# Layer 0's even pairs form and split the token difference themselves; pair 2 multiplies gate and up in turns

## The chip, the core and the metric

The kernel runs on one core of one Trainium2 chip. The metric is the device time of one execution in microseconds (us); smaller is better. The engines of the core work side by side and wait for each other by semaphores: TensorE (PE, matrix products, with its weight loads as PEld), VectorE (DVE), ScalarE (ACT), GpSimd (POOL), and SyncE (SP), which here only issues DMA transfers.

## The reference, cut to what matters

A two-layer decoder trunk on x of 512 tokens by 1024 features, all float32: a Mamba-2 mixer, a ConvFFN, shared keys and values, differential attention, a second ConvFFN. The change lies in the ConvFFN of both layers, and in one preparation for the keys that runs beside layer 0's.

```python
def causal_dwconv(u, w, b):            # width 3 over tokens
    ...
def conv_ffn(x, ln_g, up_w, conv_w, conv_b, down_w):
    u = causal_dwconv(rms_norm(x, ln_g) @ up_w, conv_w, conv_b)
    gate, up = u[..., :FFN_DIM], u[..., FFN_DIM:]
    return (jax.nn.silu(gate) * up) @ down_w      # FFN_DIM = 2816
def shared_kv(x, kv_ln_g, kv_w, k_norm_g):
    kv = rms_norm(x, kv_ln_g) @ kv_w
    ...
```

## The kernel before, in words

**Precision.** Every float32 operand is split into a high part (ACT copies it to the rounded matmul type) and a low part (DVE subtracts the high part from the value). A product is three matmuls: high by high, high by low, low by high (lines 246 to 248 for the plain products, 1437, 1439 and 1434 for layer 0's down products). The helper `pieces` (ACT at line 1083, DVE at 1084) splits a stream operand. A weight chunk is loaded to a raw buffer by SP (lines 175 and 177), its high part cast by ACT (line 185, or 1276 for down weights), its low part formed by DVE (196 or 1277). High and low weights have three buffers each. A chunk is prepared two uses ahead.

**The FFN.** The 2816 hidden columns are 22 blocks of 128, which the code calls pairs, because each has a gate block and an up block; two pairs, an even and an odd one, make a double. `PARTS_D` divides the 22 into parts of 6, 8 and 8. A part's pairs are multiplied first, and its part of the down product follows while the next part's first pairs are under way; the last part's down product ends the layer's FFN. `KINDS` says which doubles are plain (P) and which use a scheme of seven products for the up projection (S); `STEPS` is the order of the work in a part (D is the down product of the part before). In layer 0's last part the two pairs 20 and 21 come last, and the down product behind them.

**The head of an FFN.** Pairs 0 and 1 multiply the stream before it is normalised, since the norm isn't ready yet, and what comes out is scaled afterwards (`evac`, line 1468). Their weights come in two chunks, one with rows 0 to 3 of the gate and the up block, one with rows 4 to 7 of both, so that gate and up are multiplied in turns, row by row (`p < WHOLE` in `whole` and `ffn_plan`); a chunk is then loaded by two DMAs of 256 KB. From pair 2 on a chunk is a whole gate block or a whole up block, by one DMA of 512 KB: 8 rows of the gate first, then 8 rows of the up block. A row's product is the three matmuls above; its stream operands are `xgh` and `xgl`. Pair 2 is the first that needs the normalised stream, which is formed (line 1092) and split (1083, 1084) in four quarters: rows 0 and 2, 1 and 3, 4 and 6, 5 and 7. The splits write over the stream that pair 1 reads, so the quarters with rows 4 to 7 can only be split when pair 1 has used those rows.

**Behind a pair.** `tapped` forms the width-3 convolution of gate and up (ACT 1066, DVE 1068) and SiLU (ACT 1473), `gated` multiplies them (DVE 1160), and `operands` makes of a double's two results, each cut into token halves, the seven stream operands of the down product: e0 and e1 are the even pair's halves, o0 and o1 the odd pair's. Operand 0 is e0, operands 1 and 2 are o0 and o1, operand 3 is e0 - e1, operand 4 is o1 - e1, and 5 and 6 are two further sums. The even pair splits operand 0; all others are formed (lines 1314 to 1317) and split with the odd pair. For the last double of an 8-pair part they stand in the tiles sEh and sEl.

**The down product of layer 0** (`down_features`) runs the seven products in the order 5, 1, 2, 6, 7, 4, 3 (`SEVEN[0]`), which use operands 3, 0, 1, 6, 4, 5 and 2. Each has two weight chunks, and each chunk uses all doubles of the part, the last double last in each half.

**Key staging** (`stage`, called after the steps of pairs 3, 4 and 5 and after each step of the later parts but D): eight times a block of the key weights is loaded by SP to the one buffer `stage` (line 1005), scaled by ACT in two halves (1011), and stored by ACT's queue to a scratch tensor (1012). A load is asked for at one call, scaling and store two calls later, the next load two calls after that.

**Order.** PE's instructions run as they are written. The order on ACT, DVE and SP is set when the program is built, by a planner that works from estimates of its own and puts an instruction ahead of its place in the code where an engine would be free; at run time each engine and each queue works strictly in that order.

Of the kernel before, what the change touches and what calls it, by code (L numbers as in the profile page):

```python
# [31 lines left out]
PARTS_D = (0, 6), (6, 14), (14, 22)  # L32
KINDS = "PPP", "PSPP", "PPPP"
STEPS = "PPPPPPPPPPPP", "PPDPPP51P26P734PPPPP", "PPDPPPPPPPPPPPPPP"
WHOLE = 2
SEVEN = "5126743", "1257634"
AH = 8
EPS = 1e-6
# [7 lines left out]
def trunk_kernel(ctx: ExitStack, tc, x, ssm_ln_g, ssm_in_w, ssm_conv_w, ssm_conv_b, ssm_dt_bias,  # L46
# [4 lines left out]
    act, dve, pool, pe, sync = nc.scalar, nc.vector, nc.gpsimd, nc.tensor, nc.sync  # L51
# [18 lines left out]
    def w_cols(w, k0, nk, c0, ncol):  # L70
        return w[k0 * P:(k0 + nk) * P, c0:c0 + ncol].rearrange("(k p) c -> p k c", p=P), nk, ncol
# [40 lines left out]
    def down_plan(l, i):  # L112
        p0, p1 = PARTS_D[i]
        nq = (p1 - p0) // 2
        for m in SEVEN[l]:
            for c in range(0, nq, 2) if l else range(2):
                plan.append(("s%d%s_%d_%d" % (l, m, p0, c), (l, m, p0, c, min(2, nq - c) if l else nq)))

    def ffn_plan(l):
        w = ffn_up_w[l].rearrange("(k p) (j c) -> p k j c", p=P, j=2)  # L120
        for i in range(len(PARTS_D)):
            for kind, p, n in up_order(i):
                if kind == "D":
                    down_plan(l, i - 1)
                elif kind == "P" and p >= WHOLE:
                    plan.append(("h%d_%d_%d" % (l, p, n), *w_cols(ffn_up_w[l], 0, KB, n * FFN + p * P, P)))
# [110 lines left out]
    def chunk(key):  # L237
        while state["next"] <= state["use"] + AHEAD and state["next"] < len(plan):
            emit_chunk()
        state["use"] += 1  # L240
        k, h, l = ready.pop(0)
        assert k == key, (k, key)
        return h, l
# [396 lines left out]
    with tc.tile_pool(name="ssm_y", bufs=1) as yp, tc.tile_pool(name="ssm", bufs=1) as sp:  # L640
# [29 lines left out]
        with tc.issue_after(b1_end.ins):  # L670
            for c in range(NT):
# [11 lines left out]
                          in1=dtb.unsqueeze(1).to_broadcast([P, NT, NH]), op=ALU.add)  # L683
# [7 lines left out]
        for n in (13, 11, 9, 7, 5, 3):  # L691
# [6 lines left out]
                                 in1=alog.unsqueeze(1).to_broadcast([P, NT, NH]),  # L698
# [151 lines left out]
        def out_proj(g, yh, yl, norm):  # L850
            for c in range(4):
                wh, wl = chunk("out%d_%d" % (g, c))
                for i in range(2):
                    m = 2 * c + i
                    ps = mm_bank("ps_o%d_%d" % (g, m))
                    for k in range(4):
                        state["last"] = mm3(ps, wh[:, k, i * P:(i + 1) * P], wl[:, k, i * P:(i + 1) * P],
                                            yh[k], yl[k], k == 0, k == 3)
                    add_to_stream(m, ps, 16, norm)
                    yield  # L860
# [83 lines left out]
        for g in range(NG):  # L944
# [40 lines left out]
            else:  # L985
                op = out_proj(g - 1, *prev, None)
# [27 lines left out]
    def bias_ranges(pl, behind):  # L1014
        pl = pl.rearrange("p a t -> p (a t)")
        rb = pl[:AH, :32]
        pool.tensor_copy(rb[:, 0:1], behind[:AH, 0:1])
        pool.dma_start(rb, rel_bias.rearrange("b h -> h b"))
        pool.tensor_scalar(out=rb, in0=rb, scalar1=-1.0, scalar2=None, op0=ALU.mult)
        hb = NBIAS // 2  # L1020
        for i in range(2):
            bv = pl[:AH, 32 + i * hb:32 + (i + 1) * hb]
            if i:
                pool.memset(bv[:, hb - (P - 1):], FAR)
            for b, a, e in _ranges():
                a, e = max(NBIAS - e - i * hb, 0), min(NBIAS - a - i * hb, hb)
                if a < e:
                    src = rb[:, 0:e - a][:, ::-1] if b == 0 else rb[:, b:b + 1].to_broadcast([AH, e - a])
                    pool.tensor_copy(bv[:, a:e], src)
            pool.dma_start(bd[:, i * hb:(i + 1) * hb], bv)  # L1030

    def ffn(l, norm, bp, gnext, nnext):
        with (tc.tile_pool(name="ffn_h%d" % l, bufs=1) as hp, tc.tile_pool(name="ffn%d" % l, bufs=1) as fp,
# [3 lines left out]
            def whole(p, pss):  # L1037

                pss += [(aux_bank if j else mm_bank)("ps_%s%d_%d" % ("gu"[j], l, p)) for j in range(2)]
                for c in range(2):  # L1040
                    wh, wl = chunk("h%d_%d_%d" % (l, p, c))
                    if p >= WHOLE:
                        for k in range(KB):
# [30 lines left out]
            def u_tile(name):  # L1074
                return fp.tile([P, 2, T], F32, tag="u", name=name, bufs=2)
# [4 lines left out]
            sub = ALU.subtract  # L1080

            def pieces(hi, lo, v):
                act.activation(hi, v, AF.Copy)  # L1083
                dve.tensor_tensor(out=lo, in0=v, in1=hi.bitcast(F32), op=sub)  # L1084
# [74 lines left out]
            def gated(p, ga, up, sides):  # L1159
                dve.tensor_tensor(out=ga, in0=ga, in1=up, op=ALU.mult)  # L1160
                operands(p, ga, sides)
# [87 lines left out]
            def down_ahead(p0, n, ks, eng=sync):  # L1249
                for k in ks:  # L1250
                    for c in range((n // 2 + 1) // 2 if l else 2):
                        down_load(p0, n, k, c, eng)
# [40 lines left out]
            def operands(p, ga, sides):  # L1293

                h = ga.rearrange("p (i t) -> p i t", i=2)
                if p % 2 == 0:
                    if any(p == p1 - 2 and p1 - p0 == 8 for p0, p1 in PARTS_D):
                        sh, sl = (flat(t)[:, :7 * 256].rearrange("p (s t) -> p s t", s=7) for t in sE)
                    else:
                        sh = hp.tile([P, 7, 256], F32R, tag="sh", name="sh%d" % p, bufs=3)  # L1300
                        sl = hp.tile([P, 7, 256], F32R, tag="sl", name="sl%d" % p, bufs=3)
                    sides[p] = (sh, sl, h)
                    pieces(sh[:, 0], sl[:, 0], h[:, 0])
                    return
                sh, sl, e = sides[p - 1]
                pieces(sh[:, 1:3], sl[:, 1:3], h)
                e0, e1, o0, o1 = e[:, 0], e[:, 1], h[:, 0], h[:, 1]
                if l:
                    dve.tensor_tensor(out=o1, in0=e1, in1=o1, op=sub)
                    dve.tensor_tensor(out=e1, in0=e0, in1=e1, op=sub)  # L1310
                    dve.tensor_tensor(out=e0, in0=o1, in1=e0, op=sub)
                    dve.tensor_tensor(out=o0, in0=o0, in1=e0, op=ALU.add)
                else:
                    dve.tensor_tensor(out=e0, in0=e0, in1=e1, op=sub)
                    dve.tensor_tensor(out=e1, in0=o1, in1=e1, op=sub)
                    dve.scalar_tensor_tensor(out=o1, in0=o1, scalar=-1.0, in1=e0, op0=ALU.mult, op1=sub)
                    dve.scalar_tensor_tensor(out=o0, in0=o1, scalar=-1.0, in1=o0, op0=ALU.mult, op1=sub)
                pieces(sh[:, 3:5], sl[:, 3:5], e)
                pieces(sh[:, 5:7], sl[:, 5:7], h)

            def down_tokens(p0, n, sides, last):
# [149 lines left out]
            def tapped(p, us):  # L1471
                ga = taps(0, p, us[0])
                act.activation(ga, ga, AF.Silu)
                return ga, taps(1, p, us[1])
# [3 lines left out]
            def stage():  # L1478

                staged["at"] += 1  # L1480
                if staged["v"] and staged["at"] > 1:
                    key_weights_out(*staged["v"])
                    staged.update(v=None, at=0)
                elif not staged["v"] and staged["n"] < KB and staged["at"] > 1:
                    staged.update(v=key_weights_in(fp, staged["n"]), n=staged["n"] + 1, at=0)

            def plain(p, sides):

                pss = []
                for _ in whole(p, pss):  # L1490
                    yield
                sides["open"] = p, tapped(p, pss)

            def gate(sides):
                p, (ga, up) = sides.pop("open")
                gated(p, ga, up, sides)
                return ga
# [27 lines left out]
            for p in range(2, 6):  # L1525
                for _ in plain(p, sides):
                    if p > 2:
                        next(sums, None)
                        if not l:
                            stage()  # L1530
                if p == 2:
                    gated(1, *tapped(1, (u1[:, 0], u1[:, 1])), sides)
                ga = gate(sides)
                next(sums, None)
                if p == 3:
                    down_ahead(*parts[0], "z")
                if not l and p == 3:
                    bias_ranges(u_tile("ranges"), ga)
# [59 lines left out]

    norm_kv = Norm(bp, "kv")
    ffn(0, norm, bp, None, norm_kv)  # L1600


    norm1 = Norm(bp, "f1")
    with tc.tile_pool(name="att", bufs=1) as ap, ExitStack() as later:
# [353 lines left out]
        with tc.manual_schedule(engines={mybir.EngineType.PE}):  # L1958
# [49 lines left out]
            last_out(norm1)  # L2008

    ffn(1, norm1, bp, None, None)  # L2010


# [34 lines left out]
```

## Time and profile before

| | us |
|---|---|
| median of 3 runs | 1326.8 (1326.25 to 1327.58) |
| profiled execution, its own time | 1327.54 |
| its span, first to last instruction | 1325.8 |
| mean granted PE clock | 0.996 |
| busy: PE, DVE, ACT, POOL | 1310.4, 1062.4, 735.7, 173.5 |

The page gives the span, each engine's busy time, and groups of instructions by line. Waits are listed as "who waited <- for whom: us in total, times, longest". In a timeline the columns are start (us from the span's start), duration, engine, line, operation, output <- inputs, shapes, count, and in brackets the idle time before it with what ended it. Matmuls overlap in their pipeline: the work of one is the distance of two starts, not its duration. In a row of the view by stretches the columns are the stretch, its length, then busy time (and count) of PE, PEld, DVE, ACT and POOL, the granted PE clock, the DMA share and GB/s.

### The profile page before, as it was taken

How to read it: one execution, taken by the hardware profiler on the slowest of the kernel's cores; microseconds unless marked ns; L12 is line 12 of the kernel's file. 1: busy time of each engine (PE TensorE's matmuls, PEld its weight loads, DVE VectorE, ACT ScalarE, POOL GpSimd, SP SyncE). 2: the span in 40 equal slices, each digit the busy share in tenths (PEclk: the TensorE clock that was granted, in tenths of full speed). 3: DMA queues.
4: the chain of work that ended last, by engine and by line, in shares of the span. 5: the costliest groups of instructions: out<-in, count | busy, mean ns of one | idle time of the engine just before them, and what ended most of it. 6: DMA issues, size and time to landing. Idle time of an engine off the chain costs nothing.

```text
span 1325.8 us, 18563 instructions
## 1 busy us (share of the span) xinstructions
PE 1310.4 (99%) x6915; PEld 1104.2 (83%) x6915; DVE 1062.4 (80%) x1769; ACT 735.7 (55%) x1203; POOL 173.5 (13%) x204
## 2 busy tenths in 40 slices
PE   9999999999999999999999999999999999999998
PEld 8878888888887898899879888777887889888887
DVE  7889888789879976975766968677779977977776
ACT  6696554742466644643444667777556535643442
POOL 5330300200120420020011310000020020020001
PEclk9999999999999999999998999999999999999999
DMA  7553433532365796377345573221133494466335
GB/s 208 161 153 96 142 105 108 139 95 72 110 193 178 175 239 138 116 135 195 96 95 113 170 163 111 75 69 65 51 117 103 107 235 112 128 112 190 95 64 127
DMA packets 200218, 171.01 MB, mean 129 GB/s; under 512 B 7804, under 2 KB 174080, under 8 KB 200128
## 3 DMA queue, kind: packets, MB, share of 16 engines
q1 hardware_dynamic: 169424, 120.73, 30.6%
q0 software_dynamic: 27248, 43.80, 17.2%
q10 hardware_dynamic: 3456, 5.30, 1.1%
q8 instruction: 54, 0.88, 0.3%
q14 instruction: 36, 0.29, 0.1%
HBM read 163.36 MB, written 6.44 MB: 128 GB/s over the span
## 4 chain that ended last, share of the span: by engine, by line
PE 94%; DVE 2%; issue 1%; ACT 1%; DMA 0%; POOL 0%; SPq 0%; DVEq 0%; POOLq 0%; ACTq 0%
PE ps_u L246 5%; PE ps_u L247 5%; PE ps_u L248 5%; PE ps_g L247 5%; PE ps_g L248 5%; PE ps_g L246 5%; PE ps_in L246 5%; PE ps_in L248 5%; PE ps_in L247 5%; PE ps_s L1434 3%; PE ps_s L1439 3%; PE ps_s L1437 3%; PE ps_s L1333 3%; PE ps_s L1338 3%; PE ps_s L1336 3%; PE ps_o L247 2%
## 5 line engine op out<-in xcount | busy, mean ns | idle before, releaser
L196 DVE TENSOR_TENSOR wl_h<-wr_h,wh_h 128x1024 fp32r<-128x1024 f32 x80 | 98.3, 1229 | 45.2 <-ACT wh_h L185 42.5
L247 PE MATMUL ps_g<-xgl,wh_h 128*128 128x512 f32 x320 | 125.7, 393 | 3.6 <-DVE xgl L1084 3.6
L185 ACT ACTIVATE wh_h<-wr_h 128x1024 fp32r<-128x1024 f32 x80 | 84.6, 1058 | 78.1 <-PE ps_u L247 28.5
L246 PE MATMUL ps_g<-xgh,wh_h 128*128 128x512 f32 x320 | 125.6, 393 | 0.8 <-ACT xgh L1083 0.8
L248 PE MATMUL ps_g<-xgh,wl_h 128*128 128x512 f32 x320 | 125.2, 391 | 0.0
L246 PE MATMUL ps_u<-xgh,wh_h 128*128 128x512 f32 x320 | 124.6, 389 | 0.0
L247 PE MATMUL ps_u<-xgl,wh_h 128*128 128x512 f32 x320 | 124.5, 389 | 0.0
L248 PE MATMUL ps_u<-xgh,wl_h 128*128 128x512 f32 x320 | 124.5, 389 | 0.0
L246 PE MATMUL ps_in<-xgh,wh_in 128*128 128x512 f32 x304 | 122.9, 404 | 0.0
L248 PE MATMUL ps_in<-xgh,wl_in 128*128 128x512 f32 x304 | 119.7, 394 | 0.0
L247 PE MATMUL ps_in<-xgl,wh_in 128*128 128x512 f32 x304 | 119.1, 392 | 0.0
L1238 POOL DMA_DIRECT2D wz<-in_ffn_down_w_dram x36 | 44.0, 1237 | 497.9 <-DVE wl_s L1277 415.8
L247 PEld LDWEIGHTS ps_g<-xgl,wh_h 128*128 128x128 f32 x320 | 60.4, 189 | 17.1 <-DVE xgl L1084 4.9
L1276 ACT ACTIVATE wh_s<-wz 128x1024 fp32r<-128x1024 f32 (+2 forms) x42 | 41.5, 989 | 57.0 <-PE ps_s L1338 19.2
L246 PEld LDWEIGHTS ps_g<-xgh,wh_h 128*128 128x128 f32 x320 | 60.4, 189 | 13.8 <-ACT xgh L1083 1.6
L1083 ACT ACTIVATE sh<-vg 128x512 fp32r<-128x512 f32 (+1 forms) x72 | 40.3, 572 | 55.8 <-DVE vg L1160 38.3
L248 PEld LDWEIGHTS ps_g<-xgh,wl_h 128*128 128x128 f32 x320 | 60.5, 189 | 12.5
L247 PEld LDWEIGHTS ps_u<-xgl,wh_h 128*128 128x128 f32 x320 | 60.1, 188 | 12.5
L246 PEld LDWEIGHTS ps_u<-xgh,wh_h 128*128 128x128 f32 x320 | 60.2, 188 | 12.4
L248 PEld LDWEIGHTS ps_u<-xgh,wl_h 128*128 128x128 f32 x320 | 60.1, 188 | 12.4
L248 PEld LDWEIGHTS ps_in<-xgh,wl_in 128*128 128x128 f32 x304 | 57.1, 188 | 12.2 <-issue 0.4
L246 PEld LDWEIGHTS ps_in<-xgh,wh_in 128*128 128x128 f32 x304 | 57.2, 188 | 11.7 <-issue 1.3
(508 smaller groups left out, 3607.7 us busy)
## 6 DMA issues: line engine op xcount, KB each, us to landing
wr_h<-in_ffn_up_w_dram SPq DMA_DIRECT2D x72, 512.0 KB, 3.9
wr_in<-in_ssm_in_w_dram SPq DMA_DIRECT2D x40, 512.0 KB, 3.9
wz<-in_ffn_down_w_dram POOLq DMA_DIRECT2D x29, 512.0 KB, 5.9
m<-cumd POOLq DMA_DIRECT2D x16, 512.0 KB, 4.3
wr_out<-in_ssm_out_w_dram SPq DMA_DIRECT2D x16, 512.0 KB, 3.5
wr_s<-in_ffn_down_w_dram SPq DMA_DIRECT2D x13, 512.0 KB, 3.9
wr_h<-in_ffn_up_w_dram SPq DMA_DIRECT2D x16, 256.0 KB, 3.5
stage<-in_kv_w_dram SPq DMA_DIRECT2D x8, 512.0 KB, 3.9
```

Of the source, the lines that this page charges most:

```text
L185: return act.activation(self.wh[:, :self.n], self.raw[:, :self.n], AF.Copy)
L196: return eng.tensor_tensor(out=self.wl[:, :self.n], in0=self.raw[:, :self.n], in1=self.wh[:, :self.n].bitcast(F32), op=ALU.subtract)
L246: pe.matmul(ps, wh, xh, start=start, stop=False)
L247: pe.matmul(ps, wh, xl, start=False, stop=False)
L248: return pe.matmul(ps, wl, xh, start=False, stop=stop).ins
L1083: act.activation(hi, v, AF.Copy)
L1238: state["plus"] = pool.dma_start(view(t, nq), source(p0, c, nq, j, i), accum_op=ALU.add).ins
L1276: act.activation(wh[:, :n], t[:, :n], AF.Copy)
L1333: pe.matmul(pss[b], h, ws[q][1][:, cols], start=False, stop=end and q == qs[-1], skip_group_check=more)
L1336: pe.matmul(pss[b], h, ws[q][0][:, cols], start=first and q == qs[0], stop=False, skip_group_check=more)
L1338: pe.matmul(pss[b], w, ws[q][0][:, cols], start=False, stop=False, skip_group_check=more)
L1434: pe.matmul(v[:, b], wl[:, q, cols], h, start=False, stop=q == nq - 1, skip_group_check=not opens or b > 0)
```

## The change

`WHOLE` goes from 2 to 3: pair 2 of both layers takes its weights in the form of pairs 0 and 1, rows 0 to 3 of gate and up, then rows 4 to 7, multiplied in turns. In layer 0 an even pair forms e0 - e1 in place, once operand 0 is split, and splits it as operand 3; the odd pair no longer forms it and splits operand 4 alone. Layer 1's operands stay. The calls of `stage` behind pair 3's two steps go, so that each staging step comes two calls later in the code.

```diff
-WHOLE = 2
+WHOLE = 3
...
                     sides[p] = (sh, sl, h)
                     pieces(sh[:, 0], sl[:, 0], h[:, 0])
+                    if not l:
+                        dve.tensor_tensor(out=h[:, 0], in0=h[:, 0], in1=h[:, 1], op=sub)
+                        pieces(sh[:, 3], sl[:, 3], h[:, 0])
                     return
...
                 else:
-                    dve.tensor_tensor(out=e0, in0=e0, in1=e1, op=sub)
                     dve.tensor_tensor(out=e1, in0=o1, in1=e1, op=sub)
...
-                pieces(sh[:, 3:5], sl[:, 3:5], e)
+                if l:
+                    pieces(sh[:, 3:5], sl[:, 3:5], e)
+                else:
+                    pieces(sh[:, 4], sl[:, 4], e1)
                 pieces(sh[:, 5:7], sl[:, 5:7], h)
...
                     if p > 2:
                         next(sums, None)
-                        if not l:
+                        if not l and p > 3:
                             stage()
```

## The prediction, made before the changed kernel was run

> **What bounds the kernel now.** The page comes first: TensorE (PE) is busy in all but 15.4 us of the span, so only PE's gaps and the matmuls that run slowly beside them can be won.
>
> ```profile
> span 1325.8 us, 18563 instructions
> PE 1310.4 (99%) x6915; PEld 1104.2 (83%) x6915; DVE 1062.4 (80%) x1769; ACT 735.7 (55%) x1203; POOL 173.5 (13%) x204
> ```
>
> Then PE's waits (engine, line, releaser: total, times, longest):
>
> ```profile
> PE ps_s L1437 <- ACT sEh L1083: 4.8, 1, 4.8
> PE ps_g L247 <- DVE xgl L1084: 3.6, 3, 1.9
> PE ps_g L246 <- ACT xgh L1083: 0.8, 2, 0.5
> PE ps_s L1439 <- DVE sEl L1084: 0.2, 1, 0.2
> ```
>
> These are 9.4 us in two kinds of place: the last down product of layer 0, and the third pair (pair 2) of each layer. The timeline of PE shows that they cost more than their length. First the down product:
>
> ```profile
> 691.89 0.28 PE L1437 MATMUL ps_s<-sh,wh_s 128*128 128x256 f32 x1
> ...
> 697.58 0.58 PE L1437 MATMUL ps_s<-sEh,wh_s 128*128 128x256 f32 x1 [4.82 <-ACT sEh L1083]
> ...
> 699.63 0.41 PE L1437 MATMUL ps_s<-sh,wh_s 128*128 128x256 f32 x1
> 699.84 0.41 PE L1439 MATMUL ps_s<-sl,wh_s 128*128 128x256 f32 x1
> ...
> 704.51 0.29 PE L1437 MATMUL ps_s<-sh,wh_s 128*128 128x256 f32 x1
> ...
> 707.39 0.28 PE L1437 MATMUL ps_s<-sh,wh_s 128*128 128x256 f32 x1
> ...
> 710.27 0.28 PE L1437 MATMUL ps_s<-sh,wh_s 128*128 128x256 f32 x1
> ```
>
> A weight chunk is 24 matmuls here. Undisturbed it takes 710.27 - 707.39 = 2.88 us, 0.12 each. The row at 704.51 opens the second half of the second chunk, so 36 matmuls lie before it: 4.32 us of work took 12.62. **Lost: 8.30 us**, of which 4.82 and 0.23 are waits; the rest is matmuls at 0.21 instead of 0.12 for some 6 us behind the wait.
>
> Now pair 2, in layer 0 and, last two rows, in layer 1:
>
> ```profile
> 399.56 0.39 PE L246 MATMUL ps_g<-xgh,wh_h 128*128 128x512 f32 x1
> ...
> 402.84 0.50 PE L246 MATMUL ps_g<-xgh,wh_h 128*128 128x512 f32 x1 [0.29 <-ACT xgh L1083]
> 404.24 0.50 PE L247 MATMUL ps_g<-xgl,wh_h 128*128 128x512 f32 x1 [0.89 <-DVE xgl L1084]
> ...
> 407.12 0.74 PE L247 MATMUL ps_g<-xgl,wh_h 128*128 128x512 f32 x1 [1.92 <-DVE xgl L1084]
> ...
> 408.08 0.63 PE L246 MATMUL ps_g<-xgh,wh_h 128*128 128x512 f32 x1
> 408.50 0.63 PE L247 MATMUL ps_g<-xgl,wh_h 128*128 128x512 f32 x1
> ...
> 410.64 0.39 PE L246 MATMUL ps_u<-xgh,wh_h 128*128 128x512 f32 x1
> ...
> 999.10 0.39 PE L246 MATMUL ps_g<-xgh,wh_h 128*128 128x512 f32 x1
> ...
> 1006.34 0.39 PE L246 MATMUL ps_u<-xgh,wh_h 128*128 128x512 f32 x1
> ```
>
> A chunk is 24 matmuls again; what it takes undisturbed is seen in pair 4's up chunk, which isn't alternated, and in pair 1's second chunk, which multiplies gate and up in turns:
>
> ```profile
> 432.43 0.39 PE L246 MATMUL ps_u<-xgh,wh_h 128*128 128x512 f32 x1
> 437.87 0.39 PE L246 MATMUL ps_g<-xgh,wh_h 128*128 128x512 f32 x1
> ...
> 394.12 0.39 PE L246 MATMUL ps_g<-xgh,wh_h 128*128 128x512 f32 x1
> ```
>
> Both last 5.44 us (432.43 to 437.87, 394.12 to 399.56), so taking turns costs PE nothing. Pair 2's gate chunk lasted 11.08 in layer 0 and 7.24 in layer 1. **Lost: 5.64 and 1.80 us.** All that the change can win is 8.30 + 5.64 + 1.80 = 15.74 us.
>
> **The even pair's difference.** The down products of layer 0 go in the order 5, 1, 2, 6, 7, 4, 3. Product 5 takes operand 3, which needs the even pair alone, but before it is split together with operand 4, which needs the odd one. In the rows of DVE and ACT:
>
> ```profile
> 686.49 0.43 DVE L1314 TENSOR_TENSOR vg<-vg 128x256 f32<-128x256 f32 x1
> ...
> 696.38 1.15 ACT L1083 ACTIVATE sEh<-vg 128x512 fp32r<-128x512 f32 x2 [2.80 <-DVE vg L1160]
> ...
> 701.57 1.06 ACT L1276 ACTIVATE wh_s<-wx 128x1024 fp32r<-128x1024 f32 x1 [1.78 <-PE ps_s L1439]
> ```
>
> The difference (L1314) is there at 686.9, the split waits for pair 21's product (L1160) until 696.4. In the new kernel operand 3 can be split right behind L1314, and even behind the weight casts that stand there it is done by about 689, before PE arrives at 691.9. Product 1 (operand 0) is the even pair's too, so the odd pair is first wanted by product 2, after 4 chunks, at 691.9 + 11.5 = 703.4; its splits begin at 696.4 and have 6 us of room. What is late next is the weight cast of the fourth chunk (ACT at 701.57, then its low half on DVE). Before the change it waits for PE to free a buffer, which now happens 7 us earlier (about 694.3); PE wants it at 691.9 + 8.6 = 700.5. If ACT holds it behind the pair's last split, which ends about 699.4, cast and low half end at 701.6 and PE waits 0.1 to 0.5. I take 0.2: **a gain of 8.1**, bounds 7.5 and 8.3.
>
> The price is two splits of 256 columns for one of 512, in 11 double pairs of layer 0:
>
> ```profile
> L1083 ACT ACTIVATE sh<-vg 128x512 fp32r<-128x512 f32 x27 | 16.3, 625 | 21.3 <-DVE vg L1160 11.2 <-DVE vg L1317 7.1 <-DVE vg L1315 3.0
> L1083 ACT ACTIVATE sh<-vg 128x256 fp32r<-128x256 f32 x9 | 3.7, 410 | 7.7 <-DVE vg L1160 7.7
> L1084 DVE TENSOR_TENSOR sl<-vg,sh 128x512 fp32r<-128x512 f32 x27 | 18.1, 687 | 2.1 <-ACT sh L1083 1.9
> L1084 DVE TENSOR_TENSOR sl<-vg,sh 128x256 fp32r<-128x256 f32 x9 | 3.8, 421 | 1.0 <-ACT sh L1083 1.0
> ```
>
> 2 x 410 - 625 = 195 ns on ACT, 2 x 421 - 687 = 155 on DVE: 2.1 and 1.7 us over the layer. Arithmetic is only moved. The cover is the room ahead of PE, here of a weight cast in the steady part:
>
> ```profile
> 653.92 1.05 ACT L185 ACTIVATE wh_h<-wr_h 128x1024 fp32r<-128x1024 f32 x1
> ...
> 664.69 0.39 PE L246 MATMUL ps_u<-xgh,wh_h 128*128 128x512 f32 x1
> ```
>
> A cast begins when a chunk ends (653.8 here) and is for the third chunk after it (two more are ready in their buffers), so it ends 9.7 us before PE takes it. The even pair's new split waits on ACT for L1314, which waits for DVE, and behind it stand such casts; a wait of a microsecond or two there is covered. I cost it at 0; without that cover it would be the 0.4 us of the split and its wait, 11 times.
>
> **Pair 2 in turns.** Pair 2 is the first that multiplies the normalised stream, whose second half is split while the first is in use. Before, rows 4 to 7 are wanted after 12 matmuls (2.7 us), now after 24 (5.44). In layer 0 that is 405.0, and row 5's low part, the second matmul of its group, at 406.6. The DVE rows, and the weight casts that follow:
>
> ```profile
> 405.85 1.22 DVE L1084 TENSOR_TENSOR xgl<-wx,xgh 128x1024 fp32r<-128x1024 f32 x1
> ...
> 411.55 1.22 DVE L196 TENSOR_TENSOR wl_h<-wr_h,wh_h 128x1024 fp32r<-128x1024 f32 x1 [1.48 <-ACT wh_h L185]
> ...
> 435.13 1.22 DVE L196 TENSOR_TENSOR wl_h<-wr_h,wh_h 128x1024 fp32r<-128x1024 f32 x1
> ```
>
> The second xgl ends at 407.07: 0.5 us of the 5.64 stays. In layer 1 nothing stays: the wait that ended at 1004.39 was the last, and there row 5 is wanted at 1005.9. The loads become two of 256 KB for one of 512, pair 2's alone, as pairs 0 and 1 have them.
>
> But PE then runs 5.1 us ahead of a DVE that has no air:
>
> ```profile
> 411.00:436.00 25.00, 25.00 (x112) 20.68 (x111) 23.78 (x36) 18.96 (x28) 1.36 (x1) 1.00 0.61 189
> ```
>
> DVE (fourth figure) is busy 23.8 of 25 us. The cast at 435.13 is pair 5's gate; it ends at 436.35, and PE wants it with the third matmul, 437.87 + 0.45 = 438.3: a room of 1.95 us, the smallest of the stretch. With PE 5.1 ahead 3.2 are missing. DVE gets back the 1.48 it idled before 411.55 (that buffer is freed when pair 2's first chunk ends, at 405 now), and little else: a wait of 1.7 there, with the bounds 0 and 3.2. So **layer 0's head wins 5.64 - 0.5 - 1.7 = 3.4**, bounds 1.9 and 5.6; **layer 1's 1.8**. Were operand 3 still late, the first down product would now wait as the last did; the first part covers it.
>
> **Key staging.** The same 8 loads, 16 scalings and 8 stores come two steps later in the code. They run far ahead of their place (between 356 and 436 us), wherever ACT and SP are free:
>
> ```profile
> 400.50 1.34 ACT L1011 ACTIVATE stage<-stage,c 128x512 f32<-128x512 f32 x2 [3.70 <-DMA stage<-in_kv_w_dram]
> ```
>
> ACT stood 3.70 us before this one for a load, and the second half's splits stood behind it. If the move takes it away, the 0.5 above goes too and DVE gains about 1 us; if it puts such a wait ahead of a cast with less room, up to 2 are lost. Nearest to the row that moves nothing: 0.
>
> **The sum.** 8.1 + 3.4 + 1.8 = 13.3 us, bounds 9 and 15.7. The profiled execution took 1327.54 (span 1325.8 and 1.7 around it), 0.7 above the median of 1326.8; its sum gives 1314.2, and from the median 1313.5, which I take.
>
> [...] After 402.84 three waits of 3.10 us in all, the longest 1.92, left the matmuls at 0.42 instead of 0.227 until 410.64, 1.5 us more. [...]
>
> **Rivals.**
> - DVE takes the head's win back. Pair 5's wait is 3.2, with slow matmuls behind it (1.5): 5.64 - 0.5 - 3.2 - 1.5 = 0.4, total 10.3, 1316.5; with a second such wait 1319. For it speak DVE's 95%, against it the wait's own relief for DVE. Chance 0.19.
> - The wait moves within the last down product: ACT works its queue in order, and the fourth chunk's cast lands behind all splits of pair 21 and DVE's low half behind them; 3 to 4 us of wait and slow matmuls stay, 1318. Against it: ACT is idle for 2.8 us before 696.38. Chance 0.11.
> - Operand 3 is still not ready, because its split is placed with the odd pair's after all: only the heads win, 5.2 us, 1321.6. Against it: L1314 was already placed 9 us ahead. Chance 0.05.
> - Slower: the moved key staging makes ACT stand as at 400.50, 3.70 us for each of its 8 loads, all in the head, where casts have 1.95 us of room and DVE can make up nothing. Each hold is then a PE wait of 1.75 with 1.5 us of slow matmuls behind it: 8 x 3.25 = 26 us against the 13.3 won, 1339.5. It decides from the fifth hold. Against it: the four waits of ACT for these loads were 7.0 us in all, and only one met PE:
>
> ```profile
> ACT stage L1011 <- DMA stage<-in_kv_w_dram: 7.0, 4, 3.7
> ```
>
> Chance 0.06.
>
> **How the numbers follow.** The forecast (11 to 15.7 us won) has 0.59 and lies between 1311 and 1316; the range 1310.5 to 1319.5 takes in the first rival and part of the second. About 0.2% (2.7 us) is what a measurement here can tell from none: faster 0.90, within 0.04, slower 0.06.
>
> **What would show it.** Right: no wait at L1437, the first five chunks of the last down product 2.88 us apart, layer 1's pair 2 in 10.9 us. A wait of PE on wl_h L196 at pair 5 shows the DVE limit; a gate chunk of pair 2 in layer 0 still waiting over 1 us, or a wait of PE on wh_s or wl_s, would make it wrong.

## The result and the profile after

The changed kernel takes 1316.95 us (median of 6 runs, 1314.89 to 1319.12), the kernel before in the same comparison 1327.15 (6 runs, 1326.25 to 1328.08): a ratio of 0.9923 [0.991, 0.9936], 10.2 us won. The forecast was 1313.5, a win of 13.3, so 3.1 us of the win are missing: the time lies inside the range (1310.5 to 1319.5) but just outside the forecast's 1311 to 1316. The profiled execution took 1319.12, the longest of the six.

The page of the changed kernel, then its view of PE's waits:

```profile
span 1317.4 us, 18596 instructions
...
PE 1307.8 (99%) x6915; PEld 1103.0 (84%) x6915; DVE 1061.9 (81%) x1780; ACT 738.8 (56%) x1214; POOL 174.7 (13%) x204
```

```profile
PE ps_g L248 <- DVE wl_h L196: 3.0, 1, 3.0
...
PE ps_s L1341 <- DVE vu L1068: 0.4, 1, 0.4
...
PE ps_g L247 <- DVE xgl L1084: 0.3, 1, 0.3
```

The 4.8 us at the last down product are gone, and of the third pair's 4.4 us (xgl and xgh) 0.3 is left. A wait of 3.0 on the low part of a weight chunk is new, and a small one in layer 1's first down product. (Lines behind 1300 moved by up to five: 1437, 1439 and 1473 of before are 1442, 1444 and 1478 here.)

**The last down product** runs without a gap. The timeline of PE:

```profile
692.84 0.28 PE L1442 MATMUL ps_s<-sh,wh_s 128*128 128x256 f32 x1
...
693.55 0.28 PE L1442 MATMUL ps_s<-sEh,wh_s 128*128 128x256 f32 x1
...
697.15 0.28 PE L1442 MATMUL ps_s<-sh,wh_s 128*128 128x256 f32 x1
...
698.60 0.28 PE L1442 MATMUL ps_s<-sh,wh_s 128*128 128x256 f32 x1
```

From 692.84 to 698.60 lie two chunks: 5.76 us, 2.88 each. Operand 3 (sEh at 693.55) is there in time, and the timelines of ACT and DVE show why: the even pair's difference ends at 687.8, its high part at 688.7, its low part at 690.0. The fourth chunk's cast follows on ACT at 695.43, ahead of the odd pair's splits:

```profile
688.34 0.40 ACT L1083 ACTIVATE sEh<-vg 128x256 fp32r<-128x256 f32 x1
...
695.43 1.06 ACT L1276 ACTIVATE wh_s<-wx 128x1024 fp32r<-128x1024 f32 x1 [0.89 <-PE ps_s L1444]
697.81 0.63 ACT L1083 ACTIVATE sEh<-vg 128x512 fp32r<-128x512 f32 x1 [1.31 <-DVE vg L1160]
```

```profile
687.37 0.42 DVE L1305 TENSOR_TENSOR vg<-vg 128x256 f32<-128x256 f32 x1
688.47 1.23 DVE L1277 TENSOR_TENSOR wl_s<-wz,wh_s 128x1024 fp32r<-128x1024 f32 x1 [0.68 <-ACT wh_s L1276]
689.61 0.42 DVE L1084 TENSOR_TENSOR sEl<-vg,sEh 128x256 fp32r<-128x256 f32 x1
```

**The head of layer 0** wins its time and gives it back. PE at pair 2's leftover wait, and then at pair 5's gate chunk:

```profile
406.94 0.50 PE L247 MATMUL ps_g<-xgl,wh_h 128*128 128x512 f32 x1 [0.32 <-DVE xgl L1084]
...
436.33 0.80 PE L248 MATMUL ps_g<-xgh,wl_h 128*128 128x512 f32 x1 [3.01 <-DVE wl_h L196]
436.93 0.63 PE L246 MATMUL ps_g<-xgh,wh_h 128*128 128x512 f32 x1
...
442.05 0.55 PE L246 MATMUL ps_g<-xgh,wh_h 128*128 128x512 f32 x1
442.43 0.40 PE L247 MATMUL ps_g<-xgl,wh_h 128*128 128x512 f32 x1
```

From 436.33 to 442.43 PE makes 14 matmuls in 6.10 us; undisturbed they take 14 x 0.227 = 3.18. So the place costs 3.01 of wait and 2.92 of slow matmuls, 5.9 us. Matmul by matmul PE stands 5.2 us ahead of the kernel before when pair 2 is over, and 0.9 behind it after this place.

Who was late there? DVE first, then ACT:

```profile
430.35 1.22 DVE L1084 TENSOR_TENSOR sOl<-wz,sOh 128x1024 fp32r<-128x1024 f32 x1
434.45 0.69 DVE L1160 TENSOR_TENSOR vg<-vg,vu 128x512 f32<-128x512 f32 x1 [2.88 <-ACT vg L1478]
435.06 1.22 DVE L196 TENSOR_TENSOR wl_h<-wr_h,wh_h 128x1024 fp32r<-128x1024 f32 x1
```

```profile
427.24 1.06 ACT L185 ACTIVATE wh_h<-wr_h 128x1024 fp32r<-128x1024 f32 x1 [0.61 <-PE ps_g L247]
428.21 0.76 ACT L1066 ACTIVATE vg<-ps_g,cf 128x512 f32<-128x512 f32 x1
432.56 1.34 ACT L1011 ACTIVATE stage<-stage,c 128x512 f32<-128x512 f32 x2 [3.59 <-DMA stage<-in_kv_w_dram]
433.81 0.61 ACT L1478 ACTIVATE vg<-vg 128x512 f32<-128x512 f32 x1
```

Read it backwards. The weight chunk's low part (L196 at 435.06) stands on DVE behind the product of pair 3 (L1160), which waits for pair 3's SiLU (L1478 on ACT). The convolution that it takes is done at 429.8 (DVE), but in ACT's queue the last key scaling stands ahead, and its load isn't there: ACT stands for 3.59 us. There is one buffer `stage`, so a load waits for the store before it; SP could issue this one only at 426.63, and the scaling started 5.9 us later (SPq marks the issue of a transfer):

```profile
426.63 0.37 SPq L1005 DMA_DIRECT2D stage<-in_kv_w_dram  x1
```

In the kernel before, ACT had the last scaling behind the SiLU:

```profile
431.58 0.63 ACT L1473 ACTIVATE vg<-vg 128x512 f32<-128x512 f32 x1 [1.46 <-DVE vg L1068]
...
435.07 1.34 ACT L1011 ACTIVATE stage<-stage,c 128x512 f32<-128x512 f32 x2 [0.42 <-DMA stage<-in_kv_w_dram]
```

So DVE was not short of time here. It idled for 2.88 us:

```profile
411.00:436.00 25.00, 22.32 (x99) 18.16 (x97) 22.11 (x35) 17.47 (x27) 0.50 (x1) 0.99 0.73 214
```

DVE (fourth figure) was busy for 23.78 of these 25 us before the change, and for 22.11 after it.

### The profile page after: what moved, and what is told of

It is laid out like the page before. It is cut to its first block, busy times and chain, and to the rows that moved or that the text cites. A ratio compares the mean times of both kernels' runs of the same rounds, so it can differ in the third digit from the quotient of the medians.

```text
span 1317.4 us, 18596 instructions
## 1 busy us (share of the span) xinstructions
PE 1307.8 (99%) x6915; PEld 1103.0 (84%) x6915; DVE 1061.9 (81%) x1780; ACT 738.8 (56%) x1214; POOL 174.7 (13%) x204
## 4 chain that ended last, share of the span: by engine, by line
PE 95%; DVE 3%; ACT 1%; DMA 0%; issue 0%; DVEq 0%; ACTq 0%
PE ps_in L246 5%; PE ps_in L248 5%; PE ps_in L247 5%; PE ps_g L248 5%; PE ps_g L246 5%; PE ps_g L247 5%; PE ps_u L246 5%; PE ps_u L247 5%; PE ps_u L248 5%; PE ps_s L1439 3%; PE ps_s L1444 3%; PE ps_s L1442 3%; PE ps_s L1338 3%; PE ps_s L1341 3%; PE ps_s L1343 2%; PE ps_o L247 2%
## 5 line engine op out<-in xcount | busy, mean ns | idle before, releaser
L196 DVE TENSOR_TENSOR wl_h<-wr_h,wh_h 128x1024 fp32r<-128x1024 f32 x80 | 98.1, 1230 | 42.4 <-ACT wh_h L185 39.6
```

The costliest lines, as they stand in the source:

```text
L196: return eng.tensor_tensor(out=self.wl[:, :self.n], in0=self.raw[:, :self.n], in1=self.wh[:, :self.n].bitcast(F32), op=ALU.subtract)
```

## The experiments

**Theory A**: ACT is held by a key load that stands in its queue ahead of pair 3's SiLU, and moving the key staging put it there. **Its rival, theory B**, is the prediction's own term: DVE has no air in this stretch, and PE 5 us ahead must wait for it, whatever ACT does. Ratios are to the kernel before, run beside each, with 95% intervals. "None" means that the view of PE's waits lists no wait on `wl_h`.

| kernel | median, us (range; runs) | ratio | PE's wait at pair 5 |
|---|---|---|---|
| changed kernel again | 1317.26 (1314.92 to 1319.99; 5) | 0.9926 [0.9912, 0.994] | 1.96 |
| staging back in its old place | 1318.46 (1317.59 to 1320.05; 5) | 0.9939 [0.9926, 0.9951] | 2.87 |
| no staging | 1313.48 (1311.82 to 1313.9; 4) | 0.9898 [0.9884, 0.9911] | none |
| scaling tied to its place | 1313.13 (1312.38 to 1313.32; 4) | 0.9895 [0.988, 0.9911] | none |
| even pairs alone | 1318.72 (1317.56 to 1319.38; 5) | 0.9936 [0.9924, 0.9949] | none |
| turns alone | 1322.98 (1321.37 to 1323.21; 5) | 0.9967 [0.9955, 0.998] | 1.15 |
| staging move alone | 1327.02 (1326.06 to 1328.16; 11) | 1.0001 [0.9992, 1.001] | none |
| turns, scaling tied | 1320.72 (1320.32 to 1321.19; 5) | 0.9954 [0.9941, 0.9966] | 0.2 |

The kernel before took 1326.7 beside the first four and 1327.1 beside the last four.

**1. Staging back in its old place.**

```diff
-                        if not l and p > 3:
+                        if not l:
```

> The changed kernel with the key staging called as before (behind pair 3's steps too). Theory A (the load of the key block holds ACT ahead of pair 3's SiLU, and that makes PE wait 3.0 us at pair 5 and then run slowly for 2.9 us): what decides is where the planner puts the eight scalings; in the kernel before, the last one stood behind pair 4's gate convolution and waited only 0.4 us, so without the move the wait at pair 5 should be under 1 us and the time 1311 to 1313. Theory B (the move does nothing, VectorE alone is full): 1317 as with the move, PE waiting about 3 us on wl_h at pair 5.

Theory A's number for it, 1311 to 1313, was missed: 1318.46, no better than the changed kernel. But the hold itself is there again, in ACT's timeline:

```profile
429.14 0.76 ACT L1066 ACTIVATE vg<-ps_g,cf 128x512 f32<-128x512 f32 x1
433.36 1.33 ACT L1011 ACTIVATE stage<-stage,c 128x512 f32<-128x512 f32 x2 [3.46 <-DMA stage<-in_kv_w_dram]
434.60 0.61 ACT L1478 ACTIVATE vg<-vg 128x512 f32<-128x512 f32 x1
```

So the half of theory A that blamed the move falls. The planner puts the last scaling ahead of pair 3's SiLU wherever the code has it; whether the hold is what PE pays for at pair 5 is left to the next two.

**2. No staging.** The key weights' scaling by the norm's gain is left out; the keys read the weights unscaled.

```diff
 def key_weights(k0, i):
-    return ks[k0 * P:(k0 + 2) * P, i * 512:(i + 1) * 512].rearrange("(k p) c -> p k c", p=P)
+    return kv_w[k0 * P:(k0 + 2) * P, i * 512:(i + 1) * 512].rearrange("(k p) c -> p k c", p=P)
...
+                return
                 staged["at"] += 1
```

> The changed kernel without key staging: the keys' weights are read unscaled from their input, so the scaling of the key weights by the norm's gain is left out. Theory A: no hold of ACT is left, the wait at pair 5 and the 0.3 us on xgl go, 1310.5 to 1312. Theory B: VectorE has the same work, PE still waits 2 us or more on wl_h at pair 5, 1315 to 1317.

Theory A's 1310.5 to 1312 was missed by 1.5 us: 1313.48; where they lie is not shown. But PE waits nowhere in the head, and DVE's row of the same stretch tells the two theories apart:

```profile
411.00:436.00 25.00, 25.00 (x112) 20.72 (x111) 25.00 (x42) 17.23 (x25) 4.16 (x3) 1.00 0.50 128
```

DVE is now busy for all of the 25 us, and PE waits for nothing. A full DVE is no limit here.

**3. Scaling tied to its place.** All the work is kept, but a scaling may not be planned ahead of the stream split that was last written before it.

```diff
         for k in range(2):
-            act.activation(v[:, k], v[:, k], AF.Copy, scale=c2[:, 32 + k0 + k:33 + k0 + k])
+            with tc.issue_after(state["act"]):
+                act.activation(v[:, k], v[:, k], AF.Copy, scale=c2[:, 32 + k0 + k:33 + k0 + k])
...
             def pieces(hi, lo, v):
-                act.activation(hi, v, AF.Copy)
+                state["act"] = act.activation(hi, v, AF.Copy).ins
```

> The changed kernel with each scaling of a key block put behind the last split that is written before it, so that the planner can't run it ahead; the loads may still run ahead. Theory A: a load has landed long before its scaling, ACT never waits for it, and 16 scalings of 0.71 us lie where ACT is half idle: 1311 to 1312.5, close to the kernel without staging. Theory B: no change against the changed kernel, 1316 to 1318.

1313.13 (theory A's 1311 to 1312.5 was missed by 0.6), 4.1 us less than the changed kernel beside it, with intervals of the ratio that just don't meet. It computes all that the reference does, so it is the best of the versions here. The scalings now lie between 443 and 653 us. ACT's and DVE's timelines at the old place (lines are one higher in this kernel):

```profile
428.58 0.76 ACT L1067 ACTIVATE vg<-ps_g,cf 128x512 f32<-128x512 f32 x1
429.24 0.62 ACT L1479 ACTIVATE vg<-vg 128x512 f32<-128x512 f32 x1
431.46 0.63 ACT L1084 ACTIVATE sh<-vg 128x512 fp32r<-128x512 f32 x1 [1.60 <-DVE vg L1161]
```

```profile
429.62 1.21 DVE L1085 TENSOR_TENSOR sOl<-wz,sOh 128x1024 fp32r<-128x1024 f32 x1
430.75 0.68 DVE L1161 TENSOR_TENSOR vg<-vg,vu 128x512 f32<-128x512 f32 x1
431.36 1.21 DVE L196 TENSOR_TENSOR wl_h<-wr_h,wh_h 128x1024 fp32r<-128x1024 f32 x1
```

Around the cast the order on DVE is that of the changed kernel: sOl, the product, the weight chunk's low part. But sOl starts 0.7 us earlier, the 2.88 us of idle time in front of the product are gone, and the low part starts at 431.36 instead of 435.06. A hold of 3.49 us by a key load remains further on, at 530.95, where it costs PE nothing.

One thing this run leaves together: the loads move with the scalings (between 411 and 436 us the transfers fall from 214 to 126 GB/s), so it doesn't part the scaling's place in ACT's queue from the traffic of the loads. That the place is what matters is read from the chain of waits above.

**4. The changed kernel again**, beside these three, unedited.

> The changed kernel once more beside the other three, for a comparison on one chip. Both theories: 1315 to 1319, PE waiting some 3 us on wl_h at pair 5; by theory A the spread of over 3 us between its executions comes from when the key load lands and how long the matmuls behind the wait stay slow, and kernels without that wait spread by 1 us or less.

1317.26, with a hold of 2.54 and a wait of 1.96:

```profile
432.14 1.34 ACT L1011 ACTIVATE stage<-stage,c 128x512 f32<-128x512 f32 x2 [2.54 <-DMA stage<-in_kv_w_dram]
```

```profile
435.91 0.50 PE L248 MATMUL ps_g<-xgh,wl_h 128*128 128x512 f32 x1 [1.96 <-DVE wl_h L196]
...
436.83 0.63 PE L248 MATMUL ps_g<-xgh,wl_h 128*128 128x512 f32 x1
...
439.82 0.47 PE L246 MATMUL ps_g<-xgh,wh_h 128*128 128x512 f32 x1
440.12 0.40 PE L247 MATMUL ps_g<-xgl,wh_h 128*128 128x512 f32 x1
```

Eleven matmuls from 435.91 to 440.12 in 4.21 us, 1.71 more than undisturbed: 3.7 us in all, where the first profile showed 5.9. The price differs from execution to execution, and the kernel's runs spread over 5.1 us; those of the third experiment, without the hold, over 0.9. Not all of such a spread comes from the hold: without staging the runs spread over 2.1, where 1 or less was expected. And ahead of all that the change touches, the profiled executions are already apart: the matmuls of line 768 that start at 299.94 us in the kernel before start between 299.33 and 300.97 in the other nine.

**5. Even pairs alone** (`WHOLE` is 2 again, and the staging is back).

```diff
-WHOLE = 3
+WHOLE = 2
...
-                        if not l and p > 3:
+                        if not l:
```

> The kernel before with the even pair's difference alone (pair 2 not in turns, staging called as before). If the gains are separate: the whole 8.3 us of the last down product, 1318 to 1319, with the waits on xgh and xgl at pair 2 as before (4.4 us in all) and no wait at pair 5. If the early split costs other waits on ACT or VectorE: less than 7 us won, 1320 or more.

8.4 us won, as expected (matmul by matmul, 8.3 of them at the last down product); PE's waits for xgl are 3.6 us as before the change. A key load holds ACT here too, for 3.32 us at an earlier scaling (422.78 in its timeline), and DVE idles 2.59 us behind it (before 425.01). PE, which is not 5 us ahead in this kernel, doesn't wait at pair 5. So this hold cost PE nothing there, in a kernel without that lead.

**6. Turns alone** (the kernel before with `WHOLE` 3).

```diff
-WHOLE = 2
+WHOLE = 3
```

> The kernel before with pair 2 in turns alone (no early split, staging called as before). Theory A (the hold of ACT by a key load takes layer 0's 5.2 us back at pair 5): 1.8 us of layer 1 less 0.4 of a new wait there, and about -1 in layer 0: 1326 to 1327, not to be told from the kernel before. If the terms of the prediction held, 3.4 + 1.8: 1321.5.

Theory A's 1326 to 1327 was missed: 1322.98, 4.1 us won. Without the even pair's extra split the planner puts the last scaling behind the SiLU, where its hold of 1.49 us delays nothing that PE waits for. Here a wait of the kind that theory B expects does appear (PE's timeline, then the stretch):

```profile
436.01 0.50 PE L248 MATMUL ps_g<-xgh,wl_h 128*128 128x512 f32 x1 [1.15 <-DVE wl_h L196]
436.35 0.39 PE L246 MATMUL ps_g<-xgh,wh_h 128*128 128x512 f32 x1
```

```profile
411.00:436.00 25.00, 23.86 (x106) 19.42 (x104) 25.00 (x40) 18.33 (x26) 1.36 (x1) 1.00 0.67 194
```

DVE is full, and PE waits 1.15 us with no slow matmuls behind. On DVE a split and a sum stand between sOl and the cast here (0.93 us together), which come behind the cast in the second and third experiment. But a key load is at work in this run as well, earlier in the head, where a SiLU (at 405.93) stands behind the scaling in ACT's queue and DVE behind that SiLU:

```profile
401.84 1.34 ACT L1011 ACTIVATE stage<-stage,c 128x512 f32<-128x512 f32 x2 [3.98 <-DMA stage<-in_kv_w_dram]
```

```profile
406.57 0.69 DVE L1160 TENSOR_TENSOR vg<-vg,vu 128x512 f32<-128x512 f32 x1 [1.19 <-ACT vg L1473]
```

The eighth experiment has the same order on DVE around the cast and no scaling in the head, and tells the two apart.

**7. The staging move alone** (the kernel before with the diff's last edit).

```diff
-                        if not l:
+                        if not l and p > 3:
```

> The kernel before with the staging calls two steps later alone. Theory A: the planner runs the scalings far ahead whatever their place, 1326 to 1327.5. Rival: the place matters by itself, over 1 us either way.

Nothing: 1.0001 [0.9992, 1.001].

**8. Turns and the move, scaling tied** (the kernel before with `WHOLE` 3, the staging move and the edit of the third experiment; no early split).

> Pair 2 in turns with the scalings held at their place, without the early split. The last down product keeps its 8.3 us of loss; layer 0's head wins 4.8, layer 1 1.4. If operand 3 comes too late for the first down product too, now that PE is 4.8 us ahead (it had 3 us of room), PE waits 1 to 3 us at line 1437 there: 1322 to 1324 with what runs slowly behind it. If there is no such wait: 1320.5.

1320.72, 6.4 us won, as expected: the turns' share with the wait at pair 5 down to 0.2. So most of the 1.15 us of the turns alone came from the key loads, and 0.2 at most is left for theory B. The head as a whole shows why it is so small (first the kernel before, then this one):

```profile
400.00:436.00 36.00, 32.90 (x135) 26.07 (x134) 32.80 (x49) 24.62 (x35) 1.56 (x2) 0.95 0.54 171
```

```profile
400.00:436.00 36.00, 35.80 (x158) 29.34 (x157) 36.00 (x54) 22.37 (x32) 1.94 (x3) 1.00 0.34 91
```

DVE idled 3.2 of the 36 us before, in three gaps, each ended by ACT (1.05 before 405.24, 1.48 before 411.55, 0.67 before 424.74). With the scalings tied it idles nowhere in these 36 us. The last down product still waits its 4.8 us. Layer 0's first down product doesn't wait, though operand 3 is formed as late as before.

**Together.** Even pairs won 8.4, turns 4.1, the move 0.1, which is nothing: 12.6 us. The three in one kernel won 10.2 in the first comparison and 9.4 in the fourth experiment, and 13.6 with the scaling tied, run beside the latter. With either the even pairs or the turns alone the planner leaves the last scaling behind pair 3's SiLU; with both it puts it in front. That hold (3.7 us in the fourth experiment's profile) and the one in the head, behind which PE waits 0.41 at pair 2 there, make up the 4.1 between the two kernels. Why the planner orders them so is not shown.

## Why the prediction was right, and where it was wrong

- **The last down product, 8.1 us: right.** Even pairs alone won 8.4; the trace shows the two chunks at 2.88 us each, operand 3 ready at 690.0 (forecast about 689), and the fourth chunk's cast ahead of the odd pair's splits, so that even the 0.2 I held back for it was not needed.
- **Pair 2 in layer 0, 5.64 less 0.5: right.** The wait left over was 0.32 us (0.65 with the turns alone), and none in the second and third experiment.
- **Layer 1, 1.8: right at its place, 0.7 too high in all.** In PE's timeline the first matmuls of pair 2 and of pair 3 are

```profile
991.73 0.39 PE L246 MATMUL ps_g<-xgh,wh_h 128*128 128x512 f32 x1
...
1002.61 0.39 PE L246 MATMUL ps_g<-xgh,wh_h 128*128 128x512 f32 x1
```

  which is 10.88 us against 12.68 before. A new wait of 0.42 at layer 1's first down product (L1341 at 1051.69) takes some of it back, in every version with turns: matmul by matmul PE stands 9.2 us ahead of the kernel before ahead of it and 8.5 behind it, 0.7 us lost. I had no term for it.
- **Key staging, 0 for the move: right** (1.0001), but not for the whole change. The paragraph named what came, a wait put ahead of a cast with less room, at up to 2 us, and looked for it from the move alone. It came from the other two edits, which change the order around the staging, and was larger.
- **The extra splits, 0: right** as a direct cost; in the even pairs alone no wait came of them.
- **The step that failed is the wait at pair 5, "PE then runs 5.1 us ahead of a DVE that has no air", with a wait of 1.7.** The place was right, the cause and the size were not. Measured: a wait of 2.0 to 3.0 and 1.4 to 2.9 of slow matmuls, 3.7 to 5.9 us in three profiles, because ACT was held by a key load and DVE idled. Matmul by matmul the head of layer 0 won 1.1 and 0.5 us and lost 1.1 in them, instead of the 3.4 won, and below the lower bound of 1.9. Without the hold DVE works all 25 us of the stretch and costs PE 0 (second and third experiment) or 0.2 (eighth).
- **Why DVE was not the limit.** Of the 3.2 us missing, the working let DVE get back 1.48 "and little else". The two other gaps of the 3.2 that it idled between 400 and 436 us (1.05 and 0.67, both ended by ACT) go as well once no key load holds ACT, and 3.2 is just what was missing. The busy share of 95% was read as a limit, with room left in it and ahead of it.
- **The total came out inside the range in part by luck.** The 8.1 held in full and so covered a head that fell below its bounds.
- **The mechanism stood among the rivals, but for eight loads and by the move.** The last one had ACT standing 3.70 us for each of eight loads, 3.25 us of PE's time each and 26 in all. One such hold met PE at pair 5, cost 4 to 6 us, and not by the move. The first rival's 1316.5 is near the measured time, but its reason (DVE) is not the one that held.
- **An aside that falls:** "were operand 3 still late, the first down product would now wait". The eighth experiment has it late, and no wait there.

## What to carry to other kernels

An instruction that waited for a transfer held what stood behind it in its engine's order (ACT for 3.59 us; the SiLU behind it had its input at 429.8 and started at 433.81): give a helper's transfer-fed work a place behind the urgent work, or tie it there, before speeding up what runs beside it. When an engine looks full, add up its idle gaps and ask what ends each: they are room, if what it waits for can come earlier. Here DVE at 100% cost PE 0 or 0.2 us, and DVE at 88% cost it 3. Where a planner sets the order, two edits that are each good can place a third thing badly, so measure them together and apart.

## What the runs showed of the hardware

**Slow matmuls stood behind waits of 1.9 us and more, but not behind each, and the granted clock there was about half.** Behind 3.01 us of wait 13 matmuls stood about 0.43 us apart instead of 0.227, behind 2.87 six, behind 1.96 some eight, behind 1.15 none. Behind the 4.82 us at the last down product of the kernel before they stood 0.21 apart instead of 0.12. The view by stretches shows the granted PE clock of these places in two kernels. In the changed kernel it was 0.50 from 436.33 to 442.05 us, and 1.00 from 443 to 449. In the kernel before it was 0.52 from 407.12 to 410.64 and 1.00 from there to 414.20; at the last down product 0.50 from 697.58 to 703.50 and 1.00 from 705 to 711.

Nearly the same waits did not do the same. In the kernel before, waits of 0.29, 0.89 and 1.92 at pair 2 were followed by matmuls at 0.42. With the even pairs alone three such waits (0.26, 0.91 and 1.91) were followed by none:

```profile
404.49 0.51 PE L247 MATMUL ps_g<-xgl,wh_h 128*128 128x512 f32 x1 [0.91 <-DVE xgl L1084]
...
407.35 0.50 PE L247 MATMUL ps_g<-xgl,wh_h 128*128 128x512 f32 x1 [1.91 <-DVE xgl L1084]
407.68 0.39 PE L248 MATMUL ps_g<-xgh,wl_h 128*128 128x512 f32 x1
407.91 0.40 PE L246 MATMUL ps_g<-xgh,wh_h 128*128 128x512 f32 x1
```

What sets whether the slow matmuls come, and how long they last, was not shown.
